# Loading the delta output's first token part and the finished attention tiles two projection pairs sooner in a hybrid transformer layer

## The chip, the cores and the metric

One core of a Trainium2 chip runs the whole layer. The metric is the device time of one launch in microseconds; the kernel before took 2076.88 us (median of three runs, 2074.53 to 2081.3).

## The reference

One layer for 1024 prompt tokens and 8 single-token samples, width 1024, all in fp32. Two branches are computed from one input projection, a gated delta rule (output `o_a`) and a sliding-window attention (output `o_b`), and joined by per-channel gates:

```python
y_a = _gdn_out(o_a, gdn_gate, lp['gdn_onorm_w']) @ lp['w_gdn_out']
...
y_b = o_b @ lp['w_swa_out']
mix = (jax.nn.sigmoid(ga) * y_a + jax.nn.sigmoid(gb) * y_b) @ lp['w_o']
x = x + gt1 * mix
h2 = _rmsnorm(x, lp['norm2_w']) * (1 + sc2) + sh2
```

A convolutional feed-forward block and a last norm follow. The layer also returns the new states, among them the delta rule's state of every sample, S, which is 8 heads of 128x128 for each of 8 samples.

## The kernel before

Tokens lie on the free axis and are cut into three parts: part 0 (384 tokens), part 1 (384) and part 2 (264: the last 256 and the 8 samples). A weight matrix of 1024 columns is walked in eight column tiles of 128. Each product of a weight tile and a token part takes 24 matmuls: 8 slices of the inner dimension, and for each slice three matmuls (lines 180, 181, 182), since every fp32 operand is split into a high and a low half, hi x hi, hi x lo and lo x hi. So each weight tile and each token part that comes from memory is first split: ScalarE copies the high half (line 129), VectorE subtracts it to get the low half (line 130). Weight tiles have two pairs of split buffers but one landing buffer: the next tile's load (line 135) is issued once the split of the one before is done.

`branches` (line 1332) is the stage of this change. Its first half makes y_b: the attention output times `w_swa_out`, column tiles j = 0 to 7, for token parts 0 and 1 (part 2, and part 0 for tiles 3 and 4, were done in an earlier stage by `early_out`, line 1304, and lie in memory as `ubd`). Order of the (tile, part) products: (0,0), (1,0), (0,1), (1,1), (2,0), (2,1), (3,1), (4,1), (5,0), (5,1), (6,0), (6,1), (7,1), (7,0). After each product with part 1 the tile two further on is loaded. These tiles are called w0 to w7 here. `yb_out` (line 1340) multiplies each result by its gate, loaded from memory (line 1393), into the tiles `t` (three, one for each part).

The second half makes y_a: the delta output `oa` times `w_gdn_out`; its first two tiles are called w8 and w9. `oa` is loaded in three parts by `load_part` (line 1241): four DMAs each (line 1250) and four splits on ScalarE and VectorE. Part 0 has room of its own; part 2 takes the room of the samples' small tiles, part 1 that of part 1 of the attention output, so they wait for those. `ya_out` (line 1343) gates the result, adds the tile `t`, and splits the sum for the next stage.

Between the products stands `sample_delta` (line 1121), one step ahead of each: the delta rule for the 8 samples. At its end it writes a 64x128 tile to memory (line 1194, `dlr`), then for each of eight heads reads it back, broadcast over the partitions (line 1214, 512 KB, two buffers), scales it on ScalarE in eight pieces (line 1216), adds it to the head's state S on VectorE in eight pieces (line 1217), and writes S out through GpSimd's queue (line 1219). The third head's read must wait until VectorE is through with the first's.

After `branches` comes `output_pass` (line 1407): the joined branches times `w_o` in four token quarters, with the second norm of one quarter (`second_norm`, line 1479) woven into the products of the next: squares summed by TensorE (line 1496), a power on GpSimd (line 125), a diagonal tile `dg` on VectorE (line 1505) and its broadcast on TensorE (line 1506). GpSimd meanwhile combines the first feed-forward weights (`pair_weights`, lines 1577 and 1589).

The order of instructions on each engine is set at build time by a scheduler, which places each by its priority (the order of the code, moved by `weave`) and by its own estimate of when operands are ready. So an edit in one place can reorder instructions that it doesn't name, on every engine. Each engine then runs its instructions strictly in that order. `issue_after` gives an instruction an earliest place in that order.

## Time and profile before

| what | value |
|---|---|
| time, median of three runs | 2076.88 us (2074.53 to 2081.3) |
| the profiled execution's own time | 2076.01 us |
| its span, first to last instruction | 2074.3 us |
| mean granted TensorE clock | 0.993 |
| TensorE busy | 2008.0 us (97%) |
| VectorE busy | 1356.4 us (65%) |
| ScalarE busy | 902.5 us (44%) |
| DMA moved | 275.75 MB, 133 GB/s on average |

Times in the profile are microseconds from the span's first instruction; 1.7 us lie around the span. `branches` runs from about 1105 to 1283 us, the output pass follows to about 1400 us. PE is TensorE, ACT ScalarE, DVE VectorE, POOL GpSimd, SPq the queue on which SyncE issues DMAs. `out<-in` names tiles without their numbers. A row of the timeline gives the start, the length, the instruction, how many were merged (x), and in brackets how long the engine had been idle before it and for whom; DMA rows give only the time that issuing took. "PEclk" is the granted clock as a share of full speed.

### The profile page before, as it was taken

The page shows a single profiled execution, that of the slowest core. Times are in us where ns is not written, and L with a number is a line of the kernel's source. Part 1 is how long each engine was busy: PE and PEld are TensorE (multiplying, and loading weights), DVE is VectorE, ACT ScalarE, POOL GpSimd, SP SyncE. Part 2 cuts the span into 40 slices and gives each one's busy share as a digit, 9 for nine tenths or more (in the row PEclk, how much of TensorE's full clock was granted, in tenths as well). Part 3 has the DMA queues.
Part 4 walks back from the last instruction along what each step waited for, and adds up shares of the span by engine and source line. Part 5 has one row for each costly group of instructions (what it writes and reads, how often), then busy time and mean ns, then how long its engine had stood idle before and what let it go on. Part 6 is the DMA issues. An engine that isn't in the chain of part 4 may idle for free.

```text
span 2074.3 us, 41298 instructions
## 1 busy us (share of the span) xinstructions
PE 2008.0 (97%) x16245; PEld 1905.2 (92%) x16245; DVE 1356.4 (65%) x2714; ACT 902.5 (44%) x2233; POOL 522.1 (25%) x594
## 2 busy tenths in 40 slices
PE   7999999999999999989989999999999999999998
PEld 4987877799999999979989999999999999999997
DVE  4755767483655746656554575479886777668866
ACT  4664545443334343442442452345544444444443
POOL 2000000131321211211111000004556556543561
PEclk9999999999999999999999999999999999999999
DMA  8256443332322322312276774513333332388783
GB/s 293 72 145 207 138 168 116 96 99 65 82 82 57 77 69 52 91 37 61 67 198 184 253 231 133 146 58 90 105 98 103 107 95 91 126 280 280 265 285 115
DMA packets 301887, 275.75 MB, mean 133 GB/s; under 512 B 59730, under 2 KB 248111, under 8 KB 301676
## 3 DMA queue, kind: packets, MB, share of 16 engines
q1 hardware_dynamic: 295642, 252.14, 39.7%
q0 software_dynamic: 5552, 20.37, 2.8%
q8 instruction: 127, 2.08, 0.4%
q14 instruction: 68, 0.56, 0.1%
q10 hardware_dynamic: 498, 0.61, 0.1%
HBM read 212.93 MB, written 62.51 MB: 133 GB/s over the span
## 4 chain that ended last, share of the span: by engine, by line
PE 82%; DMA 6%; DVE 6%; ACT 3%; issue 1%; SPq 1%; POOL 0%; DVEq 0%; POOLq 0%; ACTq 0%
PE mm L180 18%; PE mm L181 18%; PE mm L182 18%; PE wv L180 3%; PE wv L182 3%; PE wv L181 3%; PE wy L182 2%; PE wy L180 2%; PE wy L181 2%; PE pv L652 1%; DMA raw<-in_w_swa_out_dram 1%; PE pt L190 1%; PE tp L190 1%; PE mm L264 1%; PE sc L614 1%
## 5 line engine op out<-in xcount | busy, mean ns | idle before, releaser
L180 PE MATMUL mm<-b1h,wh 128*128 128x384 f32 (+1 forms) x1520 | 496.9, 328 | 4.0 <-ACT gt L1294 1.6
L181 PE MATMUL mm<-b1l,wh 128*128 128x384 f32 (+1 forms) x1520 | 489.1, 323 | 0.0
L182 PE MATMUL mm<-b1h,wl 128*128 128x384 f32 (+1 forms) x1520 | 487.7, 323 | 0.4 <-DVE wl L130 0.3
L180 PEld LDWEIGHTS mm<-b1h,wh 128*128 128x128 f32 x1520 | 286.5, 189 | 13.1 <-issue 4.6
L181 PEld LDWEIGHTS mm<-b1l,wh 128*128 128x128 f32 x1520 | 286.8, 189 | 4.4 <-issue 4.0
L182 PEld LDWEIGHTS mm<-b1h,wl 128*128 128x128 f32 x1520 | 286.0, 188 | 4.5 <-issue 2.8
L129 ACT ACTIVATE wh<-raw 128x1024 fp32r<-128x1024 f32 x83 | 87.1, 1050 | 124.4 <-PE mm L181 72.0
L130 DVE TENSOR_TENSOR wl<-raw,wh 128x1024 fp32r<-128x1024 f32 x82 | 101.9, 1244 | 59.8 <-ACT wh L129 58.9
L181 PE MATMUL mm<-pk,w 128*128 128x260 f32 (+1 forms) x440 | 124.3, 283 | 1.1 <-DVE pk L130 1.1
L180 PE MATMUL mm<-pk,w 128*128 128x260 f32 (+1 forms) x440 | 124.3, 283 | 0.0
L182 PE MATMUL mm<-pk,w 128*128 128x260 f32 (+1 forms) x440 | 124.1, 282 | 0.0
L130 DVE TENSOR_TENSOR w<-ws,w 128x512 fp32r<-128x512 f32 x88 | 78.2, 890 | 36.0 <-ACT w L129 35.8
L1626 ACT COPY bml<-mm 128x256 f32<-128x256 f32 (+1 forms) x132 | 48.9, 371 | 97.6 <-PE mm L182 94.5
L180 PE MATMUL mm<-bmh,w 128*128 128x260 f32 (+1 forms) x320 | 90.3, 282 | 0.0
L182 PE MATMUL mm<-bmh,w 128*128 128x260 f32 (+1 forms) x320 | 90.1, 282 | 0.0
L1681 DVE SCALAR_TENSOR_TENSOR fa<-fz,fcw,fa 128x512 f32<-128x512 f32 x88 | 74.5, 867 | 18.1 <-ACT fa L1679 17.8
L180 PE MATMUL mm<-b2h,wh 128*128 128x384 f32 (+1 forms) x256 | 83.2, 328 | 3.0 <-ACT wh L129 2.9
L181 PEld LDWEIGHTS mm<-pk,w 128*128 128x128 f32 x440 | 82.8, 188 | 1.3 <-DVE pk L130 1.3
L181 PE MATMUL mm<-b2l,wh 128*128 128x384 f32 (+1 forms) x256 | 83.6, 327 | 0.4 <-DVE b2l L130 0.4
L180 PEld LDWEIGHTS mm<-pk,w 128*128 128x128 f32 x440 | 82.9, 188 | 0.2 <-ACT bml L1626 0.2
L182 PEld LDWEIGHTS mm<-pk,w 128*128 128x128 f32 x440 | 82.9, 189 | 0.0
L182 PE MATMUL mm<-b2h,wl 128*128 128x384 f32 (+1 forms) x256 | 82.9, 326 | 0.0
(645 smaller groups left out, 5889.9 us busy)
## 6 DMA issues: line engine op xcount, KB each, us to landing
raw<-in_w_in_dram SPq DMA_DIRECT2D x59, 512.0 KB
ws<-in_w_ffn_down_dram SPq DMA_DIRECT2D x55, 256.0 KB
raw<-xd SPq DMA_DIRECT2D x47, 258.0 KB
raw<-in_w_ffn_down_dram SPq DMA_DIRECT2D x47, 256.0 KB
raw<-in_w_ffn_gate_dram SPq DMA_DIRECT2D x22, 512.0 KB
raw<-in_w_ffn_up_dram SPq DMA_DIRECT2D x22, 512.0 KB
qst<-in_w_mod_dram SPq DMA_DIRECT2D x16, 512.0 KB
raw<-in_w_mod_dram SPq DMA_DIRECT2D x16, 512.0 KB
```

The costliest lines, as they stand in the source:

```text
L129: self.nc.scalar.activation(hi, x, AF.Copy)
L130: (eng or self.nc.vector).tensor_tensor(lo, x, hi.bitcast(F32), op=ALU.subtract)
L180: mm(ps, whi, xhi, start=first, stop=False, **kw)
L181: mm(ps, whi, xlo, start=False, stop=False, **kw)
L182: self.last_mm = mm(ps, wlo, xhi, start=False, stop=last, **kw).ins
L190: self.nc.tensor.transpose(out, in_, self.ident[:p, :p])
L264: nc.tensor.matmul(ps[32 * j:32 * j + 32], self.cT[:, k0 + j, :], ws[j // 2][:, j % 2, :], start=k0 == 0, stop=k0 > 0)
L614: self.scored = nc.tensor.matmul(sc[:, r, 256 - w:256], q, KH[:, lo:lo + w], start=True, stop=False)
L652: nc.tensor.matmul(pv[64 * r:64 * r + 64], V[:, n - back, ch], ps[:, r::2, :], start=back == 0, stop=back == (n > 0))
L1626: self.last_copy = nc.scalar.copy(r[p, i], x[p])
L1681: nc.vector.scalar_tensor_tensor(ai[:, c:e], zi[:, j + c:j + e], col(j), ai[:, c:e], op0=ALU.mult, op1=ALU.add)
```

## The change

In `branches` two groups of loads move two column tiles forward. The load of `oa` part 0 (four DMAs and their four splits on ScalarE and four on VectorE) follows the product (1,1) and the load of w3, where it followed (3,1) and the load of w5. The loads of the finished tiles from `ubd` (one DMA for part 2, two for the tiles 3 and 4 of part 0) follow the product (2,1) and the load of w4, where they followed (4,1) and the load of w6. Nothing is added or removed.

```diff
             if t and j < 6:
                 ws[j + 2] = weights(j + 2)
-            if t and j in (3, 4):
+            if t and j in (1, 2):
                 with self.tc.issue_after(self.w_load.ins):
-                    if j == 3:
+                    if j == 1:
                         oa = {0: self.load_part(pool2, self.oa, 0, rooms=first)}
                     else:
                         nc.sync.dma_start(ub[2], self.ubd[2].rearrange("j p n -> p j n"))
```

The scheduler's answer to it. SyncE's queue, from the load of w4 to the finished tiles: `raw_12980`, `raw_13017` and `raw_13077` are w4, w5 and w6 before, `raw_12992` is w4 now; `b2l_2035` is the landing room of `oa` part 0, `t_2040` and `t_2038` are the finished tiles.

```order
-L135 DMA raw_12980<-in_w_swa_out_dram 128x8x128
-L1393 DMA gt_13074<-sgb_2613 128x384
-L1393 DMA gt_13116<-sgb_2613 128x384
-L135 DMA raw_13017<-in_w_swa_out_dram 128x8x128
 L1250 DMA b2l_2035_12667<-oa_927 128x2x384 x4
-L1393 DMA gt_13147<-sgb_2613 128x384
-L1109 DMA out_dram<-z_13039 4x24x128 x2
-L1110 DMA out_dram<-z_13039 72x128
-L135 DMA raw_13077<-in_w_swa_out_dram 128x8x128
+L135 DMA raw_12992<-in_w_swa_out_dram 128x8x128
 L1369 DMA t_2040_12684<-ub_1873_11801 128x8x264
 L1371 DMA t_2038_12682<-ub_1874_11802 128x384 x2
```

The loads of `oa` part 0 and of the finished tiles stood behind w5 and w6; they stand now ahead of w4 and behind it.

ScalarE, where the first half of `branches` passes into the second. `b1l_2052` is the landing buffer of `dlr` (eight instructions for each head), `b2h_2109` is `oa` part 2, `b2h_2111` is `oa` part 1, `wh_13466` is w8; the row behind this piece is the split of w9 (`wh_13472`) now, while before it stood ahead of `b2h_2111`.

```order
-L1216 ACTIVATE b1l_2052_12734<-b1l_2052_12734,kq 128x128 x16
+L1216 ACTIVATE b1l_2052_12734<-b1l_2052_12734,kq 128x128 x24
 L129 ACTIVATE b2h_2109_13422<-osm 128x8x8
-L129 ACTIVATE b2h_2109_13422<-b2l_2110_13423 128x2x256
 L129 ACTIVATE wh_13466<-raw_13464 128x1024
 L129 ACTIVATE b2h_2109_13422<-b2l_2110_13423 128x2x256 x3
-L1216 ACTIVATE b1l_2052_12734<-b1l_2052_12734,kq 128x128 x16
+L1216 ACTIVATE b1l_2052_12734<-b1l_2052_12734,kq 128x128 x8
+L129 ACTIVATE b2h_2109_13422<-b2l_2110_13423 128x2x256
+L1216 ACTIVATE b1l_2052_12734<-b1l_2052_12734,kq 128x128 x8
+L129 ACTIVATE b2h_2111_13438<-b2l_2112_13439 128x768 x4
```

Three heads instead of two stand now ahead of the split of w8, and five heads instead of four ahead of what follows the first product with w8; what follows is part 1 of `oa`, then w9.

TensorE at the same place, before: `mm_13476` is the product of w8 with part 0, `mm_13509` that of w9 with part 0, `mm_13542` that of w8 with part 2.

```order
L182 MATMUL mm_13476<-b2h_2034_12666,wl_13467 128x384
L180 MATMUL mm_13509<-b2h_2034_12666,wh_13472 128x384
L181 MATMUL mm_13509<-b2l_2035_12667,wh_13472 128x384
L180 MATMUL mm_13542<-b2h_2109_13422,wh_13466 128x264
L181 MATMUL mm_13542<-b2l_2110_13423,wh_13466 128x264
```

And now, where `mm_13608` is the product of w8 with part 1:

```order
L181 MATMUL mm_13476<-b2l_2035_12667,wh_13466 128x384
L182 MATMUL mm_13476<-b2h_2034_12666,wl_13467 128x384
L180 MATMUL mm_13608<-b2h_2111_13438,wh_13466 128x384
L181 MATMUL mm_13608<-b2l_2112_13439,wh_13466 128x384
L182 MATMUL mm_13608<-b2h_2111_13438,wl_13467 128x384
```

The second product of this half needed w9; it needs part 1 of `oa` now.

The order also changes in the output pass. TensorE before and then now, around the broadcast of the first quarter's norm (`nr_15398`); `mm_14687` and `mm_14718` are the second quarter's products with tiles 2 and 3 of `w_o`:

```order
L180 MATMUL mm_14718<-bmh_2115_13458,pk_2214_14449 128x256
L1506 MATMUL nr_15398<-dg_15407,ones 128x256
L181 MATMUL mm_14718<-bml_2116_13459,pk_2214_14449 128x256
L182 MATMUL mm_14718<-bmh_2115_13458,pk_2214_14449 128x256
L180 MATMUL mm_14718<-bmh_2115_13458,pk_2214_14449 128x256
```

```order
L182 MATMUL mm_14687<-bmh_2115_13458,w_2210_14413 128x256
L1506 MATMUL nr_15398<-dg_15407,ones 128x256
L180 MATMUL mm_14718<-bmh_2115_13458,pk_2214_14449 128x256
L181 MATMUL mm_14718<-bml_2116_13459,pk_2214_14449 128x256
L182 MATMUL mm_14718<-bmh_2115_13458,pk_2214_14449 128x256
```

The broadcast stood behind 19 of the 24 matmuls of `mm_14718` and stands now ahead of all of them. Four transposes of the feed-forward state (line 190), which stood in the last product of that quarter, now stand behind the second matmul of the first quarter's last product, ahead of the broadcast. GpSimd's order is the same.

## The prediction

> **What bounds the kernel now.** The page first. Its head and the busy times:

> ```profile
> span 2074.3 us, 41298 instructions
> PE 2008.0 (97%) x16245; PEld 1905.2 (92%) x16245; DVE 1356.4 (65%) x2714; ACT 902.5 (44%) x2233; POOL 522.1 (25%) x594
> ```

> TensorE is busy 97% of the span, so the change can win only idle TensorE time, and lose by making more of it. Next, the three stretches that the moved loads leave and enter (length, then busy time of PE, PEld, DVE, ACT and POOL, granted clock, DMA share, GB/s):

> ```profile
> 1142.00:1157.00 15.00, 15.00 (x153) 14.26 (x146) 5.58 (x14) 3.16 (x6) 0.00 (x0) 1.00 0.39 112
> 1157.00:1178.00 21.00, 20.91 (x120) 19.73 (x119) 9.96 (x17) 7.24 (x10) 0.55 (x1) 1.00 0.96 304
> 1180.00:1205.00 25.00, 22.12 (x128) 21.80 (x127) 20.25 (x51) 17.42 (x45) 3.62 (x4) 0.93 1.05 366
> ```

> The loads are made in the second stretch, where the DMA engines are full (0.96) and TensorE waits for nothing; they move into the first, where the engines are 0.39 busy. TensorE loses time only in the third. What it waits for there, from the list of waits (total, times, longest) and TensorE's timeline around the second half of `branches`:

> ```profile
> PE mm L180 <- ACT wh L129: 3.3, 2, 2.9
> ```

> ```profile
> 1161.75 0.42 PE L180 MATMUL mm<-b1h,wh 128*128 128x384 f32 x1
> ...
> 1188.33 0.34 PE L180 MATMUL mm<-b2h,wh 128*128 128x384 f32 x1
> ...
> 1192.32 0.34 PE L182 MATMUL mm<-b2h,wl 128*128 128x384 f32 x1
> 1195.54 0.44 PE L180 MATMUL mm<-b2h,wh 128*128 128x384 f32 x1 [2.88 <-ACT wh L129]
> ```

> w8's first product runs from 1188.33 to 1192.66, then TensorE waits 2.88 us for the split of w9. Why that split is late stands in ScalarE's timeline:

> ```profile
> 1160.40 1.06 ACT L129 ACTIVATE wh<-raw 128x1024 fp32r<-128x1024 f32 x1 [2.11 <-DMA raw<-in_w_swa_out_dram]
> ...
> 1165.73 0.85 ACT L129 ACTIVATE b2h<-b2l 128x768 fp32r<-128x768 f32 x1 [0.16 <-DMA b2l<-oa]
> 1169.27 1.06 ACT L129 ACTIVATE wh<-raw 128x1024 fp32r<-128x1024 f32 x1 [2.68 <-DMA raw<-in_w_swa_out_dram]
> 1176.03 1.06 ACT L129 ACTIVATE wh<-raw 128x1024 fp32r<-128x1024 f32 x1 [5.70 <-DMA raw<-in_w_swa_out_dram]
> 1177.88 4.81 ACT L1216 ACTIVATE b1l<-b1l,kq 128x128 f32<-128x128 f32 x16 [0.78 <-DMA b1l<-dlr]
> 1182.59 0.24 ACT L129 ACTIVATE b2h<-osm 128x64 fp32r<-128x64 f32 x1
> ...
> 1184.06 1.04 ACT L129 ACTIVATE wh<-raw 128x1024 fp32r<-128x1024 f32 x1
> 1185.01 1.95 ACT L129 ACTIVATE b2h<-b2l 128x512 fp32r<-128x512 f32 x3
> 1188.40 2.46 ACT L1216 ACTIVATE b1l<-b1l,kq 128x128 f32<-128x128 f32 x8 [1.45 <-DMA b1l<-dlr]
> 1192.09 2.45 ACT L1216 ACTIVATE b1l<-b1l,kq 128x128 f32<-128x128 f32 x8 [1.24 <-DMA b1l<-dlr]
> 1194.45 1.04 ACT L129 ACTIVATE wh<-raw 128x1024 fp32r<-128x1024 f32 x1
> ```

> The split at 1194.45 is w9's. It stands behind the fourth head of `sample_delta` (1192.09), which came late from memory. The first product is thus not short of `oa` part 0 at all: its last split ended at 1166.58, 21.7 us before its first use at 1188.33. The finished tiles are read later still, in `ya_out`. So the move removes no wait by itself; what it does goes through the DMA queue and through the new order. SyncE's issues:

> ```profile
> 1162.75 0.40 SPq L135 DMA_DIRECT2D raw<-in_w_swa_out_dram  x1
> 1163.33 2.69 SPq L1369 DMA_DIRECT2D t<-ub  x1
> ...
> 1171.61 0.38 SPq L135 DMA_DIRECT2D raw<-in_w_swa_out_dram  x1
> 1173.85 0.80 SPq L1214 DMA_DIRECT2D b1l<-dlr  x2
> ...
> 1181.50 0.53 SPq L1214 DMA_DIRECT2D b1l<-dlr  x1
> ...
> 1184.08 0.45 SPq L1214 DMA_DIRECT2D b1l<-dlr  x1
> ```

> A head's read lands 4.0 us after its issue in the quiet (1173.85 to 1177.88), 6.9 and 8.0 us in the crowd (1181.50 to 1188.40, 1184.08 to 1192.09).

> **The change part by part.** It moves four loads of 384 KB, one of 1056 KB and two of 192 KB, together 3.0 MB, which take 8.3 us at the third stretch's 366 GB/s. The first stretch has 15 x 0.61 = 9.1 us free: they just fit, and w5, whose load is next behind them, has little to spare. Its split ended at 1161.46 and its product began at 1161.75. I charge **+0.5** (0 if all fits; 2.0 if a half of the finished tiles' 4 us still stands ahead of it). The four splits on ScalarE and VectorE move with their load into a stretch where ScalarE works 3.16 of 15 us: nothing.

> *The heads come earlier, but stand in the way of w8.* w6, issued at 1162.75, landed 6.5 us later among the moved loads; without them I give it w7's 4.4 us (1171.61 to 1176.03). So w7 follows about a microsecond sooner and the first head's scaling starts near 1176.3 instead of 1177.88. Two heads end at 1181.1 (4.81). The third head's read, issued 3.6 us after the first began (1177.88 to 1181.50), goes out at 1179.9. It used to be scaled after w8's split; it stands now ahead of it. Landing in 4.0 to 6.9 us, I take 5.0, near the quiet row, since part 2 of `oa` is now queued behind this read: 1184.9, scaled by 1187.4, then 0.24 and w8's 1.04 give its high half at 1188.7. VectorE's half takes 1.23 more:

> ```profile
> 1185.13 1.23 DVE L130 TENSOR_TENSOR wl<-raw,wh 128x1024 fp32r<-128x1024 f32 x1 [0.26 <-ACT wh L129]
> ...
> 1197.13 0.95 DVE L130 TENSOR_TENSOR b2l<-b2l,b2h 128x768 fp32r<-128x768 f32 x1
> ```

> So the low half is there at 1189.9. TensorE wants w8 at 1188.83 and its low half 0.35 later: **+0.8** (0 with 4.0 us, 2.7 with 6.9). Before, w8's split was done at 1186.36, two microseconds early.

> *The wait for w9 goes:* **-2.9**. What is late next is what now stands in its place, the product of w8 with `oa` part 1. The first product ends at 1188.83 + 0.8 + 4.2 = 1193.8. ScalarE's queue ahead of part 1's first split: w8 (to 1188.7), three pieces of part 2 (1.95, to 1190.7), the fourth head (2.45), a piece of part 2 (0.65), the fifth head (2.45), the split itself (0.85). The fifth head's read can go out only when the third is consumed, about 1187.8, now in the crowd with part 1's own 1.5 MB: landing in 6.9 to 8.0 us it comes at 1194.7 to 1195.8, is scaled by 1197.2 to 1198.3, and the split ends at 1198.0 to 1199.1. TensorE waits 4.2 to 5.3 us for the high half and about 1.1 more for low halves (0.95 each on VectorE): **+5.8**. With quiet landings of 4.0 us ScalarE's own work still sets 1190.7 + 2.45 + 0.65 + 2.45 + 0.85 = 1197.1, a wait of 3.3 + 1.1 = 4.4; that is the lower bound, 7.2 the upper, with both late by another 0.8. w9, split right after, is needed 4.2 us later and costs nothing.

> *The output pass.* Here the trace has TensorE waiting for a chain that it doesn't set: weights, GpSimd, VectorE.

> ```profile
> 1319.50 1.28 POOL L1589 TENSOR_TENSOR ws<-raw,raw 128x512 f32<-128x512 f32 x1 [40.31 <-DMA raw<-in_w_ffn_gate_dram]
> ...
> 1323.30 0.73 POOL L125 TENSOR_TENSOR rs<-rs,mhalf 128x2 f32<-128x2 f32 x1
> ```

> ```profile
> 1324.06 0.43 DVE L1505 TENSOR_TENSOR dg<-ident,rs 128x256 f32<-128x256 f32 x1 [6.14 <-POOL rs L125]
> ```

> ```profile
> 1308.53 0.28 PE L180 MATMUL mm<-bmh,pk 128*128 128x256 f32 x1
> ...
> 1308.88 0.28 PE L180 MATMUL mm<-bmh,pk 128*128 128x256 f32 x1
> ...
> 1324.54 0.70 PE L1506 MATMUL nr<-dg,ones 128*128 128x256 f32 x2 [3.05 <-DVE dg L1505]
> ```

> The power stands on GpSimd behind three operations that wait for the gate weights, and that order stays. So the broadcast comes at 1324.54 as before, but 19 matmuls of `mm_14718` that ran ahead of it now run behind: 19 x 0.117 = 2.2 us (three take 0.35), less 0.3 for the transposes that moved ahead and 0.4 for one write fewer ahead of the gate weights on SyncE: **+1.5** (0.5 to 3.0, as those weights land a microsecond sooner or 1.5 later). A wait of the first quarter's last product for its weights is covered by this one.

> *The clock.* After the 2.88 us stall it was granted at 0.66 over five microseconds, 5 x 0.34 = 1.7 us lost; after the 3.05 us stall it stayed full:

> ```profile
> 1195.00:1200.00 5.00, 4.46 (x23) 4.46 (x24) 4.66 (x7) 3.65 (x5) 0.89 (x1) 0.66 1.05 406
> 1324.00:1329.00 5.00, 4.46 (x36) 4.41 (x37) 4.30 (x8) 2.22 (x5) 0.03 (x1) 1.00 0.08 26
> ```

> I keep the first loss as it is, the new stall being longer. The second stall grows to some four microseconds; rows speak both ways, so half of 1.7: **+0.85** (0 to 1.7).

> [...]

> The sum: -2.9 + 0.5 + 0.8 + 5.8 + 1.5 + 0.85 = **+6.6 us**. From the profiled execution's 2076.01 that is 2082.6; the median of the runs stands 0.9 above that execution, so 2083.5. A measurement of this kernel tells about 0.3%, 6.2 us, from no change; the forecast lies just beyond.

> **The rivals.** *The heads land in the quiet* (ends not slower). For it: 3.0 MB leave the full stretch, and the first head landed in 4.0 us. If all heads do so from the third on, w5 and w8 cost nothing, the wait for part 1 is its lower bound and no second clock loss comes: -2.9 + 4.4 + 1.5 = +3.0, 2079.9. It decides when the fifth head lands within about 5 us. Against it: reads, states written out, w8 and `oa` still crowd 1180 to 1205 at 1.05. 0.20.

> *Part 1 is in time* (faster). If TensorE found part 1 split by 1193.8, the stall and its clock loss go, -2.9 - 1.7, with the output pass at its best +0.5: 2072.8. The fifth head would have to land within a microsecond or so of its issue; no row comes near. 0.05.

> *The move is hidden both ways.* The loads had 21.7 us to spare, so a wait of the old size re-forms where the old one was and only the output pass is felt: +1.5, 2078.4. Against it: a fifth head ahead. 0.10.

> *All at the upper ends:* -2.9 + 2.0 + 2.7 + 7.2 + 3.0 + 1.7 = +13.7, 2090.6. 0.07.

> **How the numbers follow.** The forecast has 0.58 (own range +4 to +10.5, 2081 to 2087.5), a quarter of it (0.14) below 6.2 us. Slower: 0.44 + 0.07, and 0.01 of noise, 0.52. Faster by over 0.3% no case gives; 0.03 for what I don't see. Same: the rest, 0.45. The range 2078 to 2089 leaves out the faster rival, half of the hidden move, and most of the last.

> **What would show it.** After: eight-piece heads three in a row ahead of w8's split; no wait for w9 but one of 4 to 6 us on `oa` part 1; a full DMA from 1143 instead of 1157; the broadcast at L1506 waiting longer than 3.05. Wrong if TensorE passes w8's second product without a stall, if w5 waits for more than 2 us, or if the broadcast's wait shrinks.

## The result and the profile after

The changed kernel took 2084.53 us (median of 22 runs, 2076.9 to 2093.89) against 2078.44 us (22 runs) of the kernel before beside it: ratio 1.0031, 95% interval 1.0021 to 1.0041. It is slower by about 6 us, little, but the interval leaves 1 out. A second timing (12 runs) gave 1.0026 (1.0013 to 1.0039). One run of a later timing of the kernel before, 2442.24 us at a granted clock of 0.751, is left out of that timing's ratio as a slow run.

The page of the changed kernel, head and busy times. The profiled execution took 2080.71 us, 4.7 more than that of before, and TensorE was busy 5.7 us more, with as many instructions:

```profile
span 2079.0 us, 41301 instructions
PE 2013.7 (97%) x16245; PEld 1911.6 (92%) x16245; DVE 1360.6 (65%) x2714; ACT 902.2 (43%) x2233; POOL 518.4 (25%) x594
```

Where the 4.7 us arose is read from three matmuls that both traces have: the first one of `branches` on part 1 of the attention output (A), the first one of the output pass (B), and one of the feed-forward block behind it (C). Before, and then after (start, length, instruction):

```profile
1130.91 0.61 PE L180 MATMUL mm<-b2h,wh 128*128 128x384 f32 x2
1285.02 0.49 PE L1439 MATMUL mm<-bmh,w 128*128 128x256 f32 x1 [2.06 <-ACT w L129]
1407.70 0.39 PE L181 MATMUL wv<-pk,w 128*128 128x260 f32 x1 [0.28 <-DVE pk L130]
```

```profile
1132.14 0.61 PE L180 MATMUL mm<-b2h,wh 128*128 128x384 f32 x2 [0.16 <-ACT b2h L129]
1288.64 0.50 PE L1439 MATMUL mm<-bmh,w 128*128 128x256 f32 x1 [2.06 <-ACT w L129]
1410.30 0.39 PE L181 MATMUL wv<-pk,w 128*128 128x260 f32 x1 [0.28 <-DVE pk L130]
```

After is already 1.2 us late at A, where the change has not begun to act. From A to B it loses 2.4 (156.50 against 154.11), from B to C it wins 1.0 (121.66 against 122.68), and behind C it loses the rest of the 4.7 again, about 2, in work that the change does not touch. So a single profile does not hold the whole of the result; a second one of each kernel is among the experiments.

The three stretches, as before (length, busy time of PE, PEld, DVE, ACT, POOL, granted clock, DMA share, GB/s):

```profile
1142.00:1157.00 15.00, 15.00 (x194) 14.19 (x193) 8.70 (x15) 6.54 (x11) 0.00 (x0) 1.00 0.88 273
1157.00:1178.00 21.00, 20.71 (x119) 19.81 (x119) 9.17 (x20) 4.98 (x10) 0.56 (x1) 1.00 0.65 202
1180.00:1205.00 25.00, 21.49 (x108) 20.77 (x108) 20.25 (x50) 16.42 (x42) 4.37 (x5) 0.86 1.03 363
```

The loads moved as they should: the first stretch went from 112 to 273 GB/s, the second from 304 to 202. TensorE got nothing for it; in the third its granted clock fell from 0.93 to 0.86. What it waits for between 1142 and 1283 us (total, times, longest), and its timeline at the second product:

```profile
PE mm L180 <- ACT b2h L129: 3.1, 1, 3.1
PE mm L181 <- DVE b2l L130: 0.4, 1, 0.4
PE mm L182 <- DVE wl L130: 0.3, 1, 0.3
```

```profile
1197.71 0.69 PE L180 MATMUL mm<-b2h,wh 128*128 128x384 f32 x1 [3.07 <-ACT b2h L129]
1198.85 0.69 PE L181 MATMUL mm<-b2l,wh 128*128 128x384 f32 x1 [0.45 <-DVE b2l L130]
```

The wait for w9 (2.88) is gone; in its place are 3.07 and 0.45 us for part 1 of the delta output, and matmuls that take 0.69 us, where the same form takes 0.34 us at full clock (1192.32 us in the profile before). ScalarE's timeline says why:

```profile
1176.73 4.80 ACT L1216 ACTIVATE b1l<-b1l,kq 128x128 f32<-128x128 f32 x16 [0.69 <-DMA b1l<-dlr]
1184.05 2.45 ACT L1216 ACTIVATE b1l<-b1l,kq 128x128 f32<-128x128 f32 x8 [2.52 <-DMA b1l<-dlr]
...
1186.55 1.04 ACT L129 ACTIVATE wh<-raw 128x1024 fp32r<-128x1024 f32 x1
...
1191.19 2.45 ACT L1216 ACTIVATE b1l<-b1l,kq 128x128 f32<-128x128 f32 x8 [1.27 <-DMA b1l<-dlr]
...
1194.48 2.45 ACT L1216 ACTIVATE b1l<-b1l,kq 128x128 f32<-128x128 f32 x8 [0.31 <-DMA b1l<-dlr]
1196.83 3.03 ACT L129 ACTIVATE b2h<-b2l 128x768 fp32r<-128x768 f32 x4
1201.79 1.06 ACT L129 ACTIVATE wh<-raw 128x1024 fp32r<-128x1024 f32 x1 [1.93 <-DMA raw<-in_w_gdn_out_dram]
```

Three heads, w8, a fourth and a fifth head, and only then, at 1196.83, part 1 (four splits), with w9 behind it. The heads at 1184.05, 1191.19 and 1194.48 were read by these issues of SyncE:

```profile
1179.59 0.32 SPq L1214 DMA_DIRECT2D b1l<-dlr  x1
...
1183.88 0.51 SPq L1214 DMA_DIRECT2D b1l<-dlr  x1
...
1187.23 0.33 SPq L1214 DMA_DIRECT2D b1l<-dlr  x1
```

They land 4.5, 7.3 and 7.3 us after their issue.

### The profile page after: what moved, and what is told of

Its sections match the earlier page's. It is cut to its first block, busy times and chain, and to the rows that moved or that the text cites. A ratio compares the mean times of both kernels' runs of the same rounds, so it can differ in the third digit from the quotient of the medians.

```text
span 2079.0 us, 41301 instructions
## 1 busy us (share of the span) xinstructions
PE 2013.7 (97%) x16245; PEld 1911.6 (92%) x16245; DVE 1360.6 (65%) x2714; ACT 902.2 (43%) x2233; POOL 518.4 (25%) x594
## 4 chain that ended last, share of the span: by engine, by line
PE 81%; DMA 7%; DVE 5%; ACT 3%; issue 1%; SPq 1%; POOL 1%; DVEq 0%; POOLq 0%; ACTq 0%
PE mm L180 18%; PE mm L181 18%; PE mm L182 18%; PE wv L180 2%; PE wv L182 2%; PE wv L181 2%; PE wy L180 1%; PE wy L182 1%; PE wy L181 1%; PE pv L652 1%; DMA raw<-in_w_swa_out_dram 1%; PE mm L264 1%; PE pt L190 1%; PE tp L190 1%; DMA qst<-in_w_mod_dram 1%
## 5 line engine op out<-in xcount | busy, mean ns | idle before, releaser
L180 PE MATMUL mm<-b1h,wh 128*128 128x384 f32 (+1 forms) x1520 | 497.6, 329 | 4.1 <-ACT gt L1294 1.6
L182 PE MATMUL mm<-b1h,wl 128*128 128x384 f32 (+1 forms) x1520 | 488.8, 324 | 0.3 <-DVE wl L130 0.3
L180 PEld LDWEIGHTS mm<-b1h,wh 128*128 128x128 f32 x1520 | 287.1, 189 | 13.7 <-issue 4.6
L182 PEld LDWEIGHTS mm<-b1h,wl 128*128 128x128 f32 x1520 | 286.7, 189 | 4.3 <-issue 2.8
L130 DVE TENSOR_TENSOR wl<-raw,wh 128x1024 fp32r<-128x1024 f32 x82 | 102.6, 1253 | 63.2 <-ACT wh L129 61.5
L129 ACT ACTIVATE wh<-raw 128x1024 fp32r<-128x1024 f32 x83 | 87.0, 1048 | 125.9 <-PE mm L181 73.3
L180 PE MATMUL mm<-pk,w 128*128 128x260 f32 (+1 forms) x440 | 124.7, 284 | 0.0
L182 PE MATMUL mm<-pk,w 128*128 128x260 f32 (+1 forms) x440 | 124.5, 283 | 0.0
L130 DVE TENSOR_TENSOR w<-ws,w 128x512 fp32r<-128x512 f32 x88 | 77.9, 886 | 36.8 <-ACT w L129 36.7
L180 PE MATMUL mm<-bmh,w 128*128 128x260 f32 (+1 forms) x320 | 90.3, 282 | 0.0
L182 PE MATMUL mm<-bmh,w 128*128 128x260 f32 (+1 forms) x320 | 90.0, 281 | 0.0
L180 PE MATMUL mm<-b2h,wh 128*128 128x384 f32 (+1 forms) x256 | 83.5, 329 | 3.2 <-ACT b2h L129 3.2
L181 PEld LDWEIGHTS mm<-pk,w 128*128 128x128 f32 x440 | 83.2, 189 | 1.3 <-DVE pk L130 1.3
L182 PE MATMUL mm<-b2h,wl 128*128 128x384 f32 (+1 forms) x256 | 83.5, 327 | 0.0
L180 PEld LDWEIGHTS mm<-pk,w 128*128 128x128 f32 x440 | 83.2, 189 | 0.2 <-ACT bml L1626 0.2
L182 PEld LDWEIGHTS mm<-pk,w 128*128 128x128 f32 x440 | 83.4, 190 | 0.0
```

The source lines that it names most:

```text
L129: self.nc.scalar.activation(hi, x, AF.Copy)
L130: (eng or self.nc.vector).tensor_tensor(lo, x, hi.bitcast(F32), op=ALU.subtract)
L180: mm(ps, whi, xhi, start=first, stop=False, **kw)
L181: mm(ps, whi, xlo, start=False, stop=False, **kw)
L182: self.last_mm = mm(ps, wlo, xhi, start=False, stop=last, **kw).ins
```

## The experiments

The theory (order): the early loads hurt nobody; what costs is the order that the scheduler makes of them, with three heads of `sample_delta` ahead of w8 and five ahead of part 1, so that TensorE waits longer at the second product and its clock falls for longer. The rivals: 3.0 MB more on a full bus by themselves; the exchange of w9 for part 1; chance.

One measure serves all runs: the time from A to B in the profile (before 154.11, after 156.50), which holds all of the second half of `branches`. "Half clock" counts the grid windows of 3.41 us at half speed between A and B; they are explained further below.

| kernel | ratio to before | 95% interval | waits 1142 to 1283, us | half clock | A to B, us |
|---|---|---|---|---|---|
| before, first profile | 1 | | 2.9 | 1 | 154.11 |
| before_again | 1.0008 | 0.9993 to 1.0023 | 3.1 | 1 | 153.89 |
| changed kernel | 1.0031 | 1.0021 to 1.0041 | 3.8 | 2 | 156.50 |
| after_again | 1.0026 | 1.0013 to 1.0039 | 5.3 | 2 | 158.27 |
| part0_only | 1.0016 | 1.0003 to 1.0029 | 4.5 | 1 | 155.84 |
| tiles_only | 1.0008 | 0.9993 to 1.0023 | 4.4 | 1 | 155.65 |
| w9_first | 1.0019 | 1.0007 to 1.0032 | 4.6 | 2 | 156.42 |
| heads_4_to_7_behind | 1.0005 | 0.9988 to 1.0022 | 4.2 | 2 | 156.51 |
| heads_3_to_7_behind | 1.0009 | 0.9995 to 1.0022 | 3.7 | 0 | 154.06 |
| heads_2_to_7_behind | 0.9989 | 0.9974 to 1.0004 | 0.8 | 0 | 150.27 |
| heads_behind_late_loads | 0.9989 | 0.9973 to 1.0005 | 0 | 0 | 149.33 |
| heads_behind_late_loads_again | 0.9985 | 0.9970 to 1.0000 | 1.2 | 0 | 150.69 |
| heads_2_to_7_late_loads | 1.0002 | 0.9985 to 1.0019 | 2.3 | 1 | 153.25 |

(The 2.06 us wait of the output pass's first matmul, the same in every run, is left out of the waits. Of `w9_first` and the runs below it, code has moved by two or three lines: L1441 and L1442 are L1439 before.)

**The changed kernel again**, unaltered.

> The changed kernel once more, unaltered, for a second profile and a second timing. Theory (order): five heads stand ahead of the splits of part 1, so TensorE waits 3 to 4.5 us for part 1 near 1198 us and the granted clock is low for 3 to 7 us behind that wait; the time is 4 to 8 us above the kernel before. Rival (chance): the 6 us between the medians came from stretches of low clock that fall anywhere; then the two kernels come out within 2 us of each other this time, or the profile shows the low clock at other places than before.

Its profile shows the same stall, longer (PE timeline):

```profile
1199.26 0.45 PE L180 MATMUL mm<-b2h,wh 128*128 128x384 f32 x1 [4.35 <-ACT b2h L129]
1200.25 0.69 PE L181 MATMUL mm<-b2l,wh 128*128 128x384 f32 x1 [0.55 <-DVE b2l L130]
```

The extra time is no chance: the ratio repeated, and so did the place of the stall. Its size did not: 3.5 and 4.9 us in two executions of one program.

**The kernel before again**, unaltered.

> The kernel before once more, unaltered, for a second profile. If the low clock comes in whole pieces of 3.4 us at half speed (1.7 us lost each) that any execution may or may not collect, this profile differs from the first by whole pieces ahead of 1130 us and behind 1420 us, while the wait for w9 is again 2.5 to 3.5 us with one piece behind it. If the pieces belong to the kernel, the same places show again. The ratio to the kernel before should be 1.000 with an interval of about 0.001 to either side.

Wait for w9 3.1 us, A to B 153.89, one half-clock window behind the wait: the same as the first profile there. This execution came to A 3.8 us later than the first, at 1134.7 us against 1130.9. From A to C the two profiles of before took 276.8 and 275.2 us, the two of after 278.2 and 282.9: on average 4.5 us more, most of what the two ratios say (+6.4 and +5.4 us). What lies outside A to C differs as much between two profiles of one kernel: behind C before took 666.6 and 668.8 us, after 668.7 and 670.5. Whether the change has a part in that is not shown. The ratio of before to itself, 1.0008, shows that 12 runs can't tell 0.1%.

**One half of the change at a time.** Part 0 sooner and the finished tiles as before, and the other way round:

```
-            if t and j in (1, 2):
+            if t and j in (1, 4):
```

```
-            if t and j in (1, 2):
+            if t and j in (2, 3):
...
-                    if j == 1:
+                    if j == 3:
```

> Only part 0 of the delta output is loaded sooner, the finished tiles stay where they were before. Theory (order): this half alone makes the new order (w8 with part 0, then w8 with part 1; five heads ahead of part 1's splits), so the stall of 3 to 4.5 us on part 1 and the low clock behind it are there, and the time is 3 to 8 us above the kernel before. Rival (the bus): what costs is 3.0 MB more between 1143 and 1157 us; with half of them gone the time is at most 2 us above before, and w5 doesn't wait.

> Only the finished tiles are loaded sooner, part 0 stays where it was before. Theory (order): the products keep the order of before (w8, then w9, each with part 0) with four heads ahead of the split of w9; the wait for w9 is there with 1 to 4 us, and the time is within 2 us of the kernel before. Rival (the bus): 1.4 MB ahead of w5 delay it, and the time is 1 to 3 us above before with a wait at w5.

With part 0 alone the products come in the new order, and TensorE waits for part 1 (list of waits):

```profile
PE mm L180 <- ACT b2h L129: 3.8, 1, 3.8
```

With the tiles alone they keep the order of before, and it waits for w9 (PE timeline):

```profile
1199.62 0.44 PE L180 MATMUL mm<-b2h,wh 128*128 128x384 f32 x1 [3.33 <-ACT wh L129]
```

So the load of part 0 is what turns the order, as the theory had it; its ratio, 1.0016, is about half of the whole change's. But from A to B both halves cost nearly the same (1.7 and 1.5 us over before). With the tiles alone w5 is late too, as the rival (the bus) had it:

```profile
1165.25 0.44 PE L180 MATMUL mm<-b1h,wh 128*128 128x384 f32 x1 [0.73 <-ACT wh L129]
```

With 0.29 us more for its low half (1166.51), these 1.0 us are most of that half's 1.5; its ratio, 1.0008, can't tell the theory's time from the rival's. With part 0 alone nothing waits at w5, and the low half of w8 is 0.3 us late. That w9 is still waited for with the tiles alone, longer than before, agrees with the theory's 1 to 4 us.

**w9 ahead of part 1.** The loads of the changed kernel, but w8 and w9 are loaded before part 1:

```
-        oa[1] = self.load_part(pool2, self.oa, 1)
+        wg = {0: [self.load_w(I["w_gdn_out"][0][:, j * P:(j + 1) * P]) for j in (0, 1)]}
+        with self.tc.issue_after(self.w_load.ins):
+            oa[1] = self.load_part(pool2, self.oa, 1)
...
-            w = [self.load_w(I["w_gdn_out"][0][:, j * P:(j + 1) * P]) for j in (j0, j0 + 1)]
+            w = wg.get(j0) or [self.load_w(I["w_gdn_out"][0][:, j * P:(j + 1) * P]) for j in (j0, j0 + 1)]
```

> All loads as in the changed kernel, but w9 is loaded and split ahead of part 1, so the second product is w9 with part 0 again, as before the change; five heads still stand ahead of that split. Theory (order of the heads): the fifth head's read is what is late, so TensorE waits 3 to 4.5 us for w9 as it did for part 1, with the low clock behind it, and the time is 3 to 8 us above the kernel before. Rival (the exchange of the products): part 1's four DMAs and splits are what is late; with w9 ahead of them the time is within 2 us of the kernel before.

The second product is w9 with part 0 again, and it waits 4.3 us. ScalarE:

```profile
1195.41 2.44 ACT L1216 ACTIVATE b1l<-b1l,kq 128x128 f32<-128x128 f32 x8 [0.16 <-DMA b1l<-dlr]
1197.76 1.04 ACT L129 ACTIVATE wh<-raw 128x1024 fp32r<-128x1024 f32 x1
```

The split of w9 stands right behind the fifth head and starts in the moment that this ends. The exchange of the products is not what costs; whatever comes second stands behind five heads.

**The heads moved behind.** `sample_delta` stops ahead of a given head, and the rest of it is issued behind w9 and part 1 (on top of the edit above). With heads 4 to 7 behind (heads are numbered from 0, so the fifth is head 4):

```
-            if h % 4 == 0:
+            for _ in range({0: 1, 4: 2}.get(h, 0)):
                 yield
...
-        for _ in samples:
-            pass
...
+        with self.tc.issue_after(self.w_load.ins):
+            for _ in samples:
+                pass
         self.bctx.close()
```

> All loads as in the changed kernel, w9 loaded ahead of part 1 and the last four heads of sample_delta issued behind both, so four heads instead of five stand ahead of the split of w9. Theory (order of the heads): the fifth head's 2.45 us and its late read leave the path; the wait falls from 4.3 us to about 1.5 us, the low clock behind it to one piece of 1.7 us or none; the time is 0 to 3 us below the kernel before. Rival (the loads of w9 and part 1 themselves land late): the wait stays over 3 us and the time 3 us or more above before.

For the next two, `4: 2` becomes `3: 2` and `2: 2`.

> As the last, with the fourth head behind too: three heads ahead of w8, none between w8 and part 1. Theory (order of the heads): ScalarE has w9 and part 1 split when TensorE asks; the wait there is under 1 us, no low clock behind it, and the time is 2 to 5 us below the kernel before. Rival (the heads must be done anyway): five heads, some 20 us of reads and scaling, now end later and hold up w10, the results of the second half or the room of the next stage; the wait comes back behind 1205 us with 2 us or more and the time is not below before.

> All loads as in the changed kernel; now the third head too stands behind w8 and w9, only two heads ahead. Theory (order of the heads): w8 is split by about 1183 us, its load buffer is free at once for w9, w9 is split by about 1191 us, and TensorE waits less than 1 us between 1142 and 1283 us (apart from some 0.5 us at w6), with no low clock there; the time is 2 to 6 us below the kernel before. Rival (the early loads cost by themselves): the wait stays at 2 us or more as in the run with heads 3 to 7 behind, and the time is not below before.

With the fifth head alone away the longest wait fell only to 3.4 us (4.2 in all), not to 1.5: the expectation failed. As its rival has it, w9 lands late (ScalarE waits 1.23 us for it behind the fourth head), but the rival's 3 us or more above before did not come either (1.0005). With the fourth away too the waits were 3.7 us in all (longest 1.7), still far from nothing. Of these 1.1 us are at w10 (1218.9 us) and the time is not below before, so the rival (the heads must be done anyway) is right in part. ScalarE in that run:

```profile
1187.92 2.45 ACT L1216 ACTIVATE b1l<-b1l,kq 128x128 f32<-128x128 f32 x8 [2.14 <-DMA b1l<-dlr]
...
1190.42 1.04 ACT L129 ACTIVATE wh<-raw 128x1024 fp32r<-128x1024 f32 x1
...
1198.17 1.06 ACT L129 ACTIVATE wh<-raw 128x1024 fp32r<-128x1024 f32 x1 [3.30 <-DMA raw<-in_w_gdn_out_dram]
```

No head stands between w8 (1190.42) and w9 (1198.17) any more, and yet w9 is late, this time from memory. Its load needs the one landing buffer, which the split of w8 frees, and that split stands behind the third head. The order costs at two places: the heads ahead of w9 or part 1, and the third head ahead of w8, which sends w9's load out late. With that one behind as well, and all loads as early as in the change:

```profile
1174.99 4.80 ACT L1216 ACTIVATE b1l<-b1l,kq 128x128 f32<-128x128 f32 x16 [0.76 <-DMA b1l<-dlr]
...
1181.16 1.04 ACT L129 ACTIVATE wh<-raw 128x1024 fp32r<-128x1024 f32 x1
...
1190.00 1.06 ACT L129 ACTIVATE wh<-raw 128x1024 fp32r<-128x1024 f32 x1 [1.77 <-DMA raw<-in_w_gdn_out_dram]
1191.26 4.80 ACT L1216 ACTIVATE b1l<-b1l,kq 128x128 f32<-128x128 f32 x16 [0.20 <-DMA b1l<-dlr]
1195.97 3.04 ACT L129 ACTIVATE b2h<-b2l 128x768 fp32r<-128x768 f32 x4
```

w8 is split at 1181.16, w9 at 1190.00, and no wait is left but 0.5 us at w5 and 0.3 at its low half. A to B takes 150.27 us, 6.2 less than in the changed kernel with the same loads at the same places. That decides against the bus as the main cause: with this order the early loads cost the 0.8 us at w5. (The third and fourth head stand between w9 and part 1 here, at 1191.26, and nothing waits for that.)

**Late loads with the heads behind.** The loads of the kernel before, with heads 3 to 7 behind (the scheduler then puts the third head between w8 and w9 by itself), run twice, and with heads 2 to 7 behind:

> The same order of the heads, with the loads of part 0 and of the finished tiles where the kernel before has them. Theory (order of the heads): what the change gains or loses is the order of the heads alone, so this is within 2 us of the run with five heads behind. Rival (the early loads matter by themselves): with 3.0 MB back between 1157 and 1178 us the heads and w8 land later, the wait for w9 is 2 us or more, and the time is 3 us or more above the run with five heads behind.

> The fastest kernel so far once more, unaltered. Theory: no wait between 1142 and 1283 us and no low clock there, 4.8 us less than the kernel before from these 141 us; with what other places add by chance the ratio is 0.996 to 0.999. Rival (a lucky run): the ratio is 1.000 or more and waits come back.

> The loads of the kernel before, with the third head behind w8 and w9 as well. Theory (order of the heads): w9 and part 1 are split as early as with five heads behind, so no wait there and the time within 2 us of that kernel; the heads end some 2.5 us later. Rival (the heads must be done anyway): six heads behind now hold w10 or the next stage's room, and a wait of 1 us or more appears behind 1205 us.

The first of them has nothing in its list of waits from 1142 to 1283 us but the first matmul of the output pass. It took 149.33 us from A to B, the shortest of all; run again it had a wait of 1.2 us at w9, where none was expected, and 150.69. The ratios, 0.9989 and 0.9985, point to a kernel some 2 to 3 us faster than before, but each interval reaches 1.000, so that is likely and not shown. The expectation "within 2 us of the run with five heads behind" failed: that run took 1.0009 and 154.06 us, 4.7 more from A to B. The heads came in another order than there, two ahead of w8 instead of three. With two ahead of w8 and early loads (`heads_2_to_7_behind`) it is 0.9989 and 150.27. These two orders are not quite the same either, since the third head stands behind w9 there; so the early loads cost some 1 us at most by themselves, as near as these runs tell. The last run shows the price of too much: the third to sixth head stand ahead of w10, and the sixth lands late. ScalarE, then TensorE:

```profile
1211.20 2.45 ACT L1216 ACTIVATE b1l<-b1l,kq 128x128 f32<-128x128 f32 x8 [3.24 <-DMA b1l<-dlr]
1213.55 1.04 ACT L129 ACTIVATE wh<-raw 128x1024 fp32r<-128x1024 f32 x1
```

```profile
1214.65 0.69 PE L180 MATMUL mm<-b2h,wh 128*128 128x384 f32 x1 [2.34 <-ACT wh L129]
```

Here the rival (the heads must be done anyway) was right. With the early loads the same four heads ahead of w10 held nothing up: there the third head was read right behind the load of w9 (issued 1183.91, 53.7 us behind A), here behind part 1's loads as well (1190.58, 58.1 us behind A).

## Why the prediction was right, and where not

The forecast was 2083.5 us, +6.6 by its sum; measured were +6.1 us by the medians and +6.4 by the ratio, the second time +3.7 and +5.4. The mechanism was the one that it named: three heads ahead of w8, five ahead of part 1, no gain from the earlier loads. Its steps, against the two profiles of after:

*The wait for w9 goes*, -2.9: right. *w5*, +0.5: measured 0.3 and 0.5. *w8*, +0.8: nothing; w8 was in time.

*Part 1 waits*, +5.8 (4.4 to 7.2): measured 3.07 + 0.45 = 3.5 and 4.35 + 0.55 = 4.9. This is the term that was mis-sized, by 0.9 to 2.3, in one profile below its lower bound. The third head's read went out 2.86 us after the first head's scaling began (1176.73 to 1179.59), not 3.6, and landed in 4.5, not 5.0 us. With the first head itself 0.8 us sooner than I had it (1176.73, less the 1.2 that this execution was late at A, is 1175.5, not 1176.3), the fifth head's scaling ended at 1195.7 on that scale, not at 1197.2 to 1198.3. Its landing, 7.3 us, was as forecast (6.9 to 8.0). What I had called the quiet was not quiet: the DMA engines were 0.97 busy from 1173.85 to 1177.88 in the profile before (309 GB/s), against 1.02 and 1.04 (350 and 383) over the two later reads. Why a read lands in 4.0 or in 6.9 us is not shown.

*The clock*, +0.85: this was half of a loss behind the second stall, the broadcast's, since "rows speak both ways"; there the two profiles lost nothing and 1.7 us. The loss behind the first stall I had kept as it was, and there it grew by 0.9 and 1.4 us: a term that I had put at nothing. The rows did not speak both ways; I had cut them at the wrong places. The half-speed stretches of each execution begin and end on one grid of 3.413 us: in the first profile of before they begin at 1090.59, 1196.40 and 1285.15 us, which are 31 and 26 steps apart. The windows of that grid, kernel before (length, busy time of PE first, the granted clock third from the end):

```profile
1192.99:1196.40 3.41, 0.86 (x6) 0.86 (x7) 3.07 (x9) 3.41 (x9) 0.89 (x1) 1.00 1.07 399
1196.40:1199.81 3.41, 3.41 (x17) 3.41 (x17) 3.41 (x6) 2.25 (x3) 0.00 (x0) 0.50 1.05 405
...
1319.28:1322.69 3.41, 2.21 (x19) 2.00 (x17) 0.00 (x0) 0.00 (x0) 3.11 (x3) 1.00 0.02 8
1322.69:1326.10 3.41, 1.56 (x11) 1.51 (x12) 1.45 (x5) 0.42 (x1) 1.34 (x2) 1.00 0.07 23
1326.10:1329.51 3.41, 3.41 (x31) 3.41 (x30) 3.02 (x4) 2.31 (x5) 0.00 (x0) 1.00 0.05 17
```

The wait for w9 lay almost whole in one window (busy 0.86 of 3.41), and the next ran at 0.50 from end to end. The 3.05 us wait at L1506 was longer, but a boundary cut it in two (busy 2.21 and 1.56), and the clock stayed at 1.00. At a granted clock of 0.50 a full window of 3.41 us loses 1.7 us; for one in which TensorE partly waits I take half of its busy time, an estimate. After:

```profile
1193.19:1196.60 3.41, 1.46 (x9) 1.14 (x7) 3.24 (x11) 3.10 (x11) 0.89 (x1) 1.00 1.04 390
1196.60:1200.01 3.41, 1.85 (x5) 1.46 (x6) 3.41 (x8) 3.26 (x6) 0.89 (x1) 0.50 1.09 388
1200.01:1203.42 3.41, 3.41 (x12) 3.41 (x11) 2.40 (x4) 1.06 (x1) 0.00 (x0) 0.50 1.05 393
```

The stall reached over into a second window, which was busy for 1.85 of its 3.41 us, and the one behind that was granted 0.50 as well, so two windows ran at half: 0.93 + 1.71 us lost, where before lost 1.71. The sum of these terms, -2.88 + 0.29 + 3.52 + 0.92 = +1.9, is to be held against the 2.4 us from A to B; for the second profile, -2.88 + 0.5 + 4.90 + 1.43 = +3.9 against 4.2. Taken from every run of the table in this way, waits and half-clock losses leave 149 to 150.5 us: nothing else acts in this stretch.

*The output pass*, +1.5: the step that failed. I had written that "the broadcast comes at 1324.54 as before", as if GpSimd's weights had a time of their own, and that a shrinking wait would prove me wrong. The wait had been 3.05 us in the first profile of before, and in the second:

```profile
1326.84 0.70 PE L1506 MATMUL nr<-dg,ones 128*128 128x256 f32 x2 [2.37 <-DVE dg L1505]
```

After:

```profile
1325.37 0.70 PE L1506 MATMUL nr<-dg,ones 128*128 128x256 f32 x2 [1.31 <-DVE dg L1505]
```

and in the second profile of after, with the window that follows it:

```profile
1328.94 0.88 PE L1506 MATMUL nr<-dg,ones 128*128 128x256 f32 x2 [2.60 <-DVE dg L1505]
```

```profile
1325.91:1329.32 3.41, 0.81 (x7) 0.57 (x5) 0.83 (x3) 0.00 (x0) 2.52 (x3) 1.00 0.00 1
1329.33:1332.74 3.41, 3.41 (x17) 3.33 (x16) 2.91 (x4) 1.72 (x4) 0.00 (x0) 0.50 0.23 77
```

The wait did not grow as forecast: on average it went from 2.7 to 2.0 us. The weights move with the stage. SyncE issued their load at these times, before and then after:

```profile
1310.35 0.98 SPq L1583 DMA_DIRECT2D raw<-in_w_ffn_gate_dram  x2
1313.27 0.94 SPq L1583 DMA_DIRECT2D raw<-in_w_ffn_gate_dram  x2
```

That is 25.3 and 24.6 us behind B, the stage's start; in the second profiles it is 24.3 and 24.8. The sum also contradicted itself here. Had the broadcast kept its time, with the 4.2 us of the terms ahead of it TensorE would have come to it at about 1323.8 (1321.49 + 4.2 - 2.2 + 0.3), and the wait would have swallowed most of these 4.2 us; the sum adds them in full.

Counted from B, the broadcast comes 39.5 and 38.2 us later in the two profiles of before, 36.7 and 38.2 in those of after. From the broadcast to C, in the first profiles, after takes 84.9 us where before takes 83.2: the 19 matmuls did move behind it, at about 1.7 us. Over the whole pass, B to C, before took 122.7 and 121.4, after 121.7 and 124.6 us. These hold one, no, one and two half-clock windows of 1.7 us; without them it is 121.0 and 121.4 before, 119.9 and 121.2 after. So the order of this pass costs nothing that can be told; the +1.1 us by which after is longer on average are windows, one of them behind the 2.60 us wait.

That the total came out so near is in part luck. From A to C these steps came to +4.5 us on average, where the sum has +6.6. Part 1 was put too high, the second half-clock window at nothing, the output pass at +1.5 for a reason that was wrong, and the rest of the measured difference, 1 to 2 us, is not found between A and C, where all the terms of the forecast lie. The rival "the heads land in the quiet" did not come true: the fifth head would have had to land within about 5 us and took 7.3. From A to B its terms make +1.5 and the forecast's +4.2; measured were +2.4 and +4.2.

## What to carry to other kernels

The load that was moved earlier won nothing here, its data having been split 21.7 us before its first use; look in such a case at what the scheduler does with the queues that the move changes, because there the time is won or lost: here a few copies whose results TensorE does not wait for, ahead of the splits that it does wait for, were worth 3 to 8 us between A and B with the same loads. Judge a small change from the stretch between two instructions that both traces share, with two profiles of each kernel, and take the rest of the span for chance until it repeats.

## What the runs showed of the hardware

From these shares, as an estimate for this stretch: a wait of up to about 1.4 us (0.40 of a window) in otherwise busy work costs only itself; one of 2 to 3 us costs 1.7 us more or not by where it falls on the grid (the 2.06 us wait of the output pass's first matmul did in the first profile of before, and did not in the second); and a stall over some 4 us costs it always, and a part of a second window where it reaches over. This is most of the scatter of this kernel: executions of one program differ by whole windows (one near 1415 us is at half speed in the second profile of before and in the first of after, and not in the other of either kernel), and the mean clock of the changed kernel's runs goes with their time (0.993 in the shortest of 2076.9 us, 0.984 in the longest of 2093.89). With each run's clock loss taken off, the standard deviation of its 22 runs falls from 4.4 to 1.8 us.
